# Input and output products of a state-space scan on narrow strips of TensorE: issued together, and copied out of PSUM, inside a one-core encoder block

## The chip, the cores and the metric

The kernel runs on one core of one Trainium2 chip. The metric is the device time in microseconds (us) of one execution. The kernel before was run three times; the median of these runs stands for it. One further execution was taken with the hardware profiler, and all rows below are from that one.

## The reference, cut to what matters

One layer of an encoder with 256 tokens and a width of 2048: a combined input projection feeds three mixers (chunked attention, a diagonal complex state-space scan called S5, and an mLSTM), whose gated results go through an output projection; then come cross-attention to a memory and a SwiGLU block. Everything is float32. The change touches the S5 branch:

```python
u = h[...].reshape(l, 48, 16)                  # 48 groups of 16 channels
bu_r = einsum('lgn,gpn->lgp', u, bbr)          # input products: 16 channels -> 64 states
bu_i = einsum('lgn,gpn->lgp', u, bbi)
x[t] = a * x[t-1] + bu[t]                      # complex, diagonal, over the 256 tokens
y = einsum('lgp,gnp->lgn', xr, c_re) - einsum('lgp,gnp->lgn', xi, c_im)   # output products
y = gelu(y + d_skip * u); y = y * sigmoid(y @ w_glu + b_glu)
```

## The kernel before

The large products (`gemm_i`, `gemm_ii`) are float32 emulated with two float32r parts. For each 1 MB piece of weights SyncE (SP) issues a load into one of two buffers (`raw`); ScalarE casts 1024 columns at a time to `whi` (L116), VectorE computes the rest `wlo` (L117), and TensorE multiplies three times per k-tile (L146 to L148, or L169 to L171 for transposed results). `whi` and `wlo` have four buffers each. These steps have the highest priority of the planner (`WPRI`); evacuations of products have the next one (`EPRI`); all else is ordered by its place in the text.

The S5 branch runs beside that, as a generator (`s5_gen`, L400) from which `run(bg_gen, n)` (L755 to L798) takes one step at a time between the products of the first phase. Its steps: 48 groups are 24 pairs; a pair has 128 states, one per partition. Six chunks `c` hold four pairs `j` each. For a pair, VectorE builds the table `E` of rotations (six operations, L372 to L377), TensorE makes two input products from 32 rows (L422, real and imaginary, each on the row strip `q = 32 * j` of the array) into one PSUM tile of the tag `sm`, VectorE rotates them straight from PSUM (L428, L429, into `s2k` scratch), adds and subtracts (L430, L431), scans (L435, twice) and rotates back into the tile `xx` (L440 to L443; four buffers). After four pairs TensorE makes the eight output products of the chunk (L449): 128 rows to 32 columns, real (`i = 0`) and imaginary (`i = 1`), each pair on its own column strip, and all in one PSUM tile `py`; L451 adds the result to `u`. The output products are asked for in the order `i`, then `j = 0, 1, 2, 3`. After the last chunk `s5_glu` (L454) makes the operand `yg` from `u`.

The tag `sm` has four PSUM banks, which all transposes, the mLSTM and the attention share. TensorE's queue is a fixed list that the planner wrote when the kernel was built: between the large products stand those of the three mixers, where the planner expected their inputs. A float32 product (not float32r) shows in the trace as two records: 48 input products are 96 records on L422, 48 output products 96 records on L449.

Of the kernel before, what the change touches and what calls it, by code (L numbers as in the profile page):

```python
# [14 lines left out]
ALU = mybir.AluOpType  # L15
# [23 lines left out]
# columns of the array of per-partition parameters  # L39
# [8 lines left out]
# columns of the array of constants: identity, ones, mask of the mLSTM  # L48
# [4 lines left out]
def tile_block(ctx: ExitStack, tc: tile.TileContext, a: dict, out: bass.AP):  # L53
# [26 lines left out]
    def junk(tag, n=512):  # L80
        """somewhere for an output that only its sum is wanted of"""
        t = scr.tile([P, 512], BF16, tag=tag, name=nm(tag), bufs=1)
        return t[:, :n]
# [22 lines left out]
    def dma_after(dst, src):  # L106
        """a load that comes behind the weights asked for so far"""
        with tc.issue_after(last_w[0]):
            nc.sync.dma_start(dst, src)
# [10 lines left out]
    def gemm_i(xh, xl, nk, src, off, n, evac, first=None):  # L120
        """acc[tok, n] = x @ w; w comes from the flat array src at off, in blocks [P, 4, n]."""
# [35 lines left out]
    def gemm_ii(xh, xl, nk, src, off, evac, raw=None):  # L157
        """acc[n, tok] = (x @ w)^T for 128 columns of w, in one block [P, nk, 128]."""
        po = acc()[:, :T]
        if raw is None:  # L160
            raw = load_w(src[off:off + P * nk * P].rearrange("(p f) -> p f", p=P), nk * P)
        k = 0
        while k < nk:
            kk = min(8, nk - k)
            hi, lo = split_w(raw, k * P, (k + kk) * P)
            for j in range(kk):
                kt = k + j
                h = hi[:, j * P:(j + 1) * P]
                PE.matmul(po, h, xh[:, kt, :], start=(kt == 0), stop=False)  # L169
                PE.matmul(po, h, xl[:, kt, :], start=False, stop=False)  # L170
                PE.matmul(po, lo[:, j * P:(j + 1) * P], xh[:, kt, :], start=False,  # L171
                          stop=(kt == nk - 1))
            k += kk
        evac(po)
        return off + P * nk * P

# [18 lines left out]
    def rstd_of(dst, ss, n, r=None):  # L195
        """dst = (ss / n + eps) ^ -0.5 (* r, one factor per partition)"""
        w = dst.shape[1]
        G.tensor_scalar(dst, ss, 1.0 / n, EPS, ALU.mult, ALU.add)
        G.tensor_tensor(dst, dst, mhalf[:, 0:w], ALU.pow)
        if r is not None:  # L200
            G.tensor_scalar(dst, dst, r, None, ALU.mult)

    def split_act(hi, lo, src, g=None):
        """hi + lo = src * g, exactly up to float32."""
# [7 lines left out]
    def transposes(dst, srcs):  # L212
        """dst [P, len * 128] in PSUM: each src [rows, 128] transposed."""
        for i, s in enumerate(srcs):
            PE.transpose(dst[:, i * P:(i + 1) * P], s, ident)  # L215
# [8 lines left out]
    # the tensor engine's clock rises while it waits for the first loads  # L224
# [12 lines left out]
    def load_x(k, n=0):  # L237
        """what is wanted of x before the weights of k-tiles k .. k+n-1 of the first product"""
# [20 lines left out]
    def vexp(dst, src, n):  # L259
# [12 lines left out]
        # 2^k in two factors  # L272
# [12 lines left out]
    # =====================  S5  =====================  # L285
# [25 lines left out]
    def s5_params():  # L311
# [5 lines left out]
        # reduce the angle to [-pi, pi]  # L317
# [10 lines left out]
        # (a - 1) / lambda  # L328
# [50 lines left out]
    def powers(tb, c1, s1):  # L379
        """tb[:, :, j, t] = (cos, sin) of t * angle, t < 16; returns nothing."""  # L380
# [4 lines left out]
        for n, m in ((2, 1), (3, 2), (5, 4), (9, 7)):  # L385
            # entries n .. n+m-1 are those 1 .. m turned by entry n-1
# [7 lines left out]
    def s5_powers():  # L394
        powers(eb, sp(CS), sp(SNN))
        # angle of 16 steps: step 15 turned by one more
# [3 lines left out]
    def s5_gen():  # L400
        """the scan, pair of groups by pair of groups; yields after each step of work"""
        for c in range(6):
            js = slice(4 * c, 4 * c + 4)
            xs = []
            for j in range(4):
                jj = 4 * c + j
# [10 lines left out]
                q = 32 * j  # L417
                cb = E[:, 0].unsqueeze(1).to_broadcast([P, 2, T])
                sb_ = E[:, 1].unsqueeze(1).to_broadcast([P, 2, T])
                pb = sm()  # L420
                for i in range(2):
                    PE.matmul(pb[:, i * T:(i + 1) * T], bT[q:q + 32, i, c, :], u[q:q + 32, c, :],  # L422
                              start=True, stop=True, tile_position=(q, 0))
# [3 lines left out]
                w, tm = s2k(), s2k()  # L427
                V.tensor_tensor(two(w), two(pb), cb, ALU.mult)  # L428
                V.tensor_tensor(two(tm), two(pb), sb_, ALU.mult)  # L429
# [7 lines left out]
                xx = s5.tile([P, 512], F32, tag="xx", name=nm("xx"), bufs=4)  # L437
                xs.append(xx)
# [7 lines left out]
            for i in range(2):  # L446
                for j in range(4):
                    q = 32 * j
                    PE.matmul(py[q:q + 32, :], cT[:, i, 4 * c + j, :], xs[j][:, i * T:(i + 1) * T],  # L449
                              start=(i == 0), stop=(i == 1), tile_position=(0, q))  # L450
# [20 lines left out]
    # =====================  mLSTM  =====================  # L471
# [23 lines left out]
    def mqk(h):  # L495
        """q^T and k^T of head h, [e, tok]"""
# [26 lines left out]
    def m_gates():  # L523
        """decays of the mLSTM: a (tok-major), -c (rows), exp(-m) (tok-major)"""
# [27 lines left out]
        V.tensor_tensor(rows[:, 0], rows[:, 1], rows[:, 2], ALU.subtract)      # a  # L552
        V.tensor_tensor_scan(rows[:, 3], on, rows[:, 0], NEG, ALU.mult, ALU.max)  # c
        V.tensor_tensor(rows[:, 1], rows[:, 2], rows[:, 3], ALU.add)           # m
# [68 lines left out]
    # =====================  chunked attention  =====================  # L623
# [60 lines left out]
    # =====================  gates and branches  =====================  # L684
# [3 lines left out]
    def gate(b, n, dst):  # L688
        """sigmoid of the gate's pre-activation, branch b, columns of chunk n, into dst(t)"""
# [37 lines left out]
    # us  # L727
# [9 lines left out]
    # xm  # L737
# [10 lines left out]
    # vm, with the input and forget gates beside head 0  # L748
# [7 lines left out]
    # attention and om  # L756
# [18 lines left out]
    # gates and branches m and a  # L775
# [30 lines left out]
    def to_operand(srcs, dh, dl, k0, gname=None):  # L806
        """srcs: two tiles [128 tok, 512]; their transpose goes to k-tiles k0 .. k0+3"""
# [26 lines left out]
    # =====================  output projection, residual  =====================  # L834
# [41 lines left out]
    # =====================  keys and values of the memory  =====================  # L876
# [4 lines left out]
    def norm_head(po, r, n):  # L881
        """RMS-normalised rows of po * r (r a per-row factor), without the gain"""
# [28 lines left out]
    # x1 operand  # L911
# [12 lines left out]
    # =====================  cross attention  =====================  # L924
# [71 lines left out]
    # =====================  SwiGLU  =====================  # L996
# [34 lines left out]
def _rows(w, widths):  # L1031
    """w [K, N] -> flat: for each run of columns, for each 4 k-tiles, a block [128, 4, n]."""
# [13 lines left out]
def _cols(w):  # L1046
    """w [K, N] -> flat: for each 128 columns, a block [128, K / 128, 128]."""
# [4 lines left out]
def _prep(i):  # L1052
# [15 lines left out]
    # per head [128, q|k, 2, 256]  # L1068
# [8 lines left out]
    # relative-position bias, [q, head, (q tile 0: keys 0..127 | q tile 1: keys 0..255)]  # L1077
# [31 lines left out]
    def pairs(v):  # L1109
        """[48, 64, 16] -> block-diagonal over pairs of groups [128, 24, 32]"""  # L1110
# [25 lines left out]
```

## Time and profile before

| | us |
|---|---|
| median of 3 runs | 2051.26 |
| lowest, highest | 2050.34, 2051.73 |
| span of the profiled execution | 2048.7 |
| TensorE busy in it | 2039.7 |
| VectorE busy | 1251.7 |
| ScalarE busy | 966.0 |

The span runs from the first to the last instruction of the profiled execution. The S5 branch issues its first input product at 172.5 us and its last output product at 714.8 us; its operand `yg` is first multiplied at 759 us. A busy TensorE is one that has a matmul in flight; matmuls overlap, so the time that an instruction costs is read from its start to the start of the next one, not from its duration. TensorE's granted clock is 1.00 in all of these stretches, the upper of its two levels.

### The profile page before, as it was taken

What the parts mean: (1) busy time and instruction counts of PE and PEld (TensorE: products, weight loads), DVE (VectorE), ACT (ScalarE), POOL (GpSimd) and SP (SyncE); (2) the same over time, 40 slices, a digit from 0 to 9 for tenths busy, and PEclk for the clock granted to TensorE, in tenths of its full rate; (3) what the DMA queues carried; (4) which work ended last, traced back from release to release, by engine and by line L of the source; (5) the groups of instructions that cost most, each with busy time, mean ns of one, the idle gap of its engine ahead of it and who ended that gap; (6) DMA issues with size and microseconds to landing.
All of it is one profiled execution on the core that took longest, in us unless ns stands there. A gap on an engine that the chain in (4) does not pass through costs nothing.

```text
span 2048.7 us, 25114 instructions
## 1 busy us (share of the span) xinstructions
PE 2039.7 (100%) x9880; PEld 1670.9 (82%) x9880; DVE 1251.7 (61%) x1804; ACT 966.0 (47%) x1308; POOL 73.7 (4%) x142
## 2 busy tenths in 40 slices
PE   9999999999999999999999999999999999999999
PEld 7998888777777788888888888888888888888887
DVE  7967885769887857645544655445444444444443
ACT  8555556544344445554544545444444444433332
POOL 1001202000000000011000100000000000000000
PEclk9999999999999999999999999999999999999999
DMA  8555455445555555765555444555555555555553
GB/s 309 186 174 165 152 179 186 155 172 174 180 183 188 192 171 195 271 218 175 175 185 185 144 145 164 185 185 185 185 185 185 185 185 185 185 185 195 195 197 132
DMA packets 60406, 377.78 MB, mean 184 GB/s; under 512 B 6912, under 2 KB 8064, under 8 KB 18816
## 3 DMA queue, kind: packets, MB, share of 16 engines
q1 hardware_dynamic: 56880, 367.42, 51.4%
q0 software_dynamic: 2112, 6.82, 1.2%
q10 hardware_dynamic: 1296, 1.95, 0.3%
q8 instruction: 77, 1.26, 0.2%
q14 instruction: 41, 0.34, 0.1%
HBM read 374.06 MB, written 2.10 MB: 184 GB/s over the span
## 4 chain that ended last, share of the span: by engine, by line
PE 99%; DVE 0%; DMA 0%; issue 0%; SPq 0%; ACT 0%; DVEq 0%; ACTq 0%
PE acc L146 29%; PE acc L148 29%; PE acc L147 28%; PE acc L169 2%; PE acc L170 2%; PE acc L171 2%; PE sm L422 1%; PE sm L812 1%; PE sm L952 1%; PE sm L978 1%; PE sm L449 1%; PE sm L215 0%; PE sm L896 0%; DMA raw<-in_w_in_dram 0%; DVE xT_l L210 0%
## 5 line engine op out<-in xcount | busy, mean ns | idle before, releaser
L117 DVE TENSOR_TENSOR wlo<-raw,whi 128x1024 fp32r<-128x1024 f32 (+2 forms) x700 | 834.7, 1194 | 697.7 <-ACT whi L116 694.3
L116 ACT CAST whi<-raw 128x1024 fp32r<-128x1024 f32 (+2 forms) x700 | 715.9, 1025 | 941.3 <-PE acc L148 816.9
L146 PE MATMUL acc<-whi,x2T_h 128*128 128x512 f32 x704 | 281.2, 399 | 0.0
L148 PE MATMUL acc<-whi,x2T_l 128*128 128x512 f32 x704 | 277.9, 395 | 0.0
L147 PE MATMUL acc<-wlo,x2T_h 128*128 128x512 f32 x704 | 277.2, 394 | 0.0
L147 PE MATMUL acc<-wlo,xT_h 128*128 128x512 f32 (+2 forms) x704 | 264.6, 377 | 1.8 <-DVE wlo L117 1.6
L148 PE MATMUL acc<-whi,xT_l 128*128 128x512 f32 (+2 forms) x704 | 265.3, 378 | 0.0
L146 PE MATMUL acc<-whi,xT_h 128*128 128x512 f32 (+2 forms) x704 | 262.4, 377 | 0.2
L148 PEld LDWEIGHTS acc<-whi,x2T_l 128*128 128x128 f32 x704 | 132.2, 188 | 33.4
L147 PEld LDWEIGHTS acc<-wlo,x2T_h 128*128 128x128 f32 x704 | 132.2, 188 | 31.4
L146 PEld LDWEIGHTS acc<-whi,x2T_h 128*128 128x128 f32 x704 | 132.2, 188 | 30.1
L147 PEld LDWEIGHTS acc<-wlo,xT_h 128*128 128x128 f32 x704 | 132.0, 188 | 29.8 <-DVE wlo L117 3.3
L146 PEld LDWEIGHTS acc<-whi,xT_h 128*128 128x128 f32 x704 | 131.5, 188 | 29.6 <-issue 3.2
L148 PEld LDWEIGHTS acc<-whi,xT_l 128*128 128x128 f32 x704 | 132.1, 188 | 27.8 <-issue 1.9
L146 PE MATMUL acc<-whi,hT_h 128*128 128x512 f32 x352 | 139.1, 395 | 0.0
L147 PE MATMUL acc<-wlo,hT_h 128*128 128x512 f32 x352 | 139.1, 395 | 0.0
L148 PE MATMUL acc<-whi,hT_l 128*128 128x512 f32 x352 | 139.0, 395 | 0.0
L148 PE MATMUL acc<-whi,eT_l 128*128 128x512 f32 x256 | 101.6, 397 | 0.0
L147 PE MATMUL acc<-wlo,eT_h 128*128 128x512 f32 x256 | 101.4, 396 | 0.0
L146 PE MATMUL acc<-whi,eT_h 128*128 128x512 f32 x256 | 101.2, 395 | 0.0
L169 PE MATMUL acc<-xT_h,whi 128*128 128x256 f32 x352 | 99.9, 284 | 0.0
L170 PE MATMUL acc<-xT_l,whi 128*128 128x256 f32 x352 | 99.5, 283 | 0.0
(375 smaller groups left out, 2837.0 us busy)
## 6 DMA issues: line engine op xcount, KB each, us to landing
raw<-in_w_gu_dram SPq DMA_DIRECT2D x88, 1024.0 KB, 4.8
raw<-in_w_in_dram SPq DMA_DIRECT2D x68, 1024.0 KB, 4.8
raw<-in_w_down_dram SPq DMA_DIRECT2D x44, 1024.0 KB, 4.7
raw<-in_w_xkv_dram SPq DMA_DIRECT2D x32, 1024.0 KB, 4.7
raw<-in_w_ii_dram SPq DMA_DIRECT2D x22, 1024.0 KB, 5.0
raw<-in_w_out_dram SPq DMA_DIRECT2D x16, 1024.0 KB, 5.0
raw<-in_w_xq_dram SPq DMA_DIRECT2D x16, 1024.0 KB, 4.8
raw<-in_w_xo_dram SPq DMA_DIRECT2D x16, 1024.0 KB, 4.8
```

The lines of the kernel that those rows point to most:

```text
L116: S.copy(hi[:, :n], raw[:, c0:c1])
L117: V.tensor_tensor(lo[:, :n], raw[:, c0:c1], hi[:, :n].bitcast(F32), ALU.subtract)
L146: PE.matmul(o, sh, h, start=(kt == 0), stop=False)
L147: PE.matmul(o, sh, lw, start=False, stop=False)
L148: PE.matmul(o, xl[:, kt, t * P:(t + 1) * P], h, start=False, stop=(kt == nk - 1))
L169: PE.matmul(po, h, xh[:, kt, :], start=(kt == 0), stop=False)
L170: PE.matmul(po, h, xl[:, kt, :], start=False, stop=False)
L171: PE.matmul(po, lo[:, j * P:(j + 1) * P], xh[:, kt, :], start=False, stop=(kt == nk - 1))
L422: PE.matmul(pb[:, i * T:(i + 1) * T], bT[q:q + 32, i, c, :], u[q:q + 32, c, :], start=True, stop=True, tile_position=(q, 0))
L449: PE.matmul(py[q:q + 32, :], cT[:, i, 4 * c + j, :], xs[j][:, i * T:(i + 1) * T], start=(i == 0), stop=(i == 1), tile_position=(0, q))
L812: PE.transpose(px[:, j * T + t * P:j * T + (t + 1) * P], srcs[t][:, (kp + j) * P:(kp + j + 1) * P], ident)
L952: PE.matmul(pS[:, t * T:(t + 1) * T], qx[:, qi, d, t * P:(t + 1) * P], kx[:, ki, d], start=(d + i == 0), stop=(d == 3 and i == 2))
```

## The change

For every second pair (`j` = 0 and 2) the input products of this pair and of the next one are now issued together: four products, real ones of both pairs, then imaginary ones of both, on two neighbouring row strips and into two PSUM tiles. ScalarE copies both tiles to SBUF, into two buffers of `xx`, which are now taken here and not after the scan. VectorE then rotates from and into this SBUF tile; the `s2k` scratch tile `w` is gone. The output products get the priority `EPRI`, and the pairs are asked for in the order 3, 2, 1, 0. No load, no wait by hand and no other line is changed (the rest of the diff takes out comments).

```diff
         for c in range(6):
-            js = slice(4 * c, 4 * c + 4)
             xs = []
             for j in range(4):
+                if j % 2 == 0:
+
+                    pb = [sm(), sm()]
+                    for i in range(2):
+                        for e in range(2):
+                            q = 32 * (j + e)
+                            PE.matmul(pb[e][:, i * T:(i + 1) * T], bT[q:q + 32, i, c, :],
+                                      u[q:q + 32, c, :], start=True, stop=True,
+                                      tile_position=(q, 0))
+                    for e in range(2):
+                        xx = s5.tile([P, 512], F32, tag="xx", name=nm("xx"), bufs=4)
+                        S.copy(xx, pb[e])
+                        xs.append(xx)
                 jj = 4 * c + j
...
-                q = 32 * j
                 cb = E[:, 0].unsqueeze(1).to_broadcast([P, 2, T])
                 sb_ = E[:, 1].unsqueeze(1).to_broadcast([P, 2, T])
-                pb = sm()
-                for i in range(2):
-                    PE.matmul(pb[:, i * T:(i + 1) * T], bT[q:q + 32, i, c, :], u[q:q + 32, c, :],
-                              start=True, stop=True, tile_position=(q, 0))
...
-                w, tm = s2k(), s2k()
-                V.tensor_tensor(two(w), two(pb), cb, ALU.mult)
-                V.tensor_tensor(two(tm), two(pb), sb_, ALU.mult)
+                w, tm = xs[j], s2k()
+                V.tensor_tensor(two(tm), two(w), sb_, ALU.mult)
+                V.tensor_tensor(two(w), two(w), cb, ALU.mult)
...
-                xx = s5.tile([P, 512], F32, tag="xx", name=nm("xx"), bufs=4)
-                xs.append(xx)
+                xx = xs[j]
...
             py = sm()[:, :T]
-            for i in range(2):
-                for j in range(4):
-                    q = 32 * j
-                    PE.matmul(py[q:q + 32, :], cT[:, i, 4 * c + j, :], xs[j][:, i * T:(i + 1) * T],
-                              start=(i == 0), stop=(i == 1), tile_position=(0, q))
+            with tc.high_priority(offset=EPRI):
+                for i in range(2):
+                    for j in (3, 2, 1, 0):
+                        q = 32 * j
+                        PE.matmul(py[q:q + 32, :], cT[:, i, 4 * c + j, :],
+                                  xs[j][:, i * T:(i + 1) * T], start=(i == 0), stop=(i == 1),
+                                  tile_position=(0, q))
```

## Rows read from the trace of the kernel before

**Rows 1.** The page: busy time of each engine (share of the span, instructions), and the chain of work that ended last, by engine.

```profile
PE 2039.7 (100%) x9880; PEld 1670.9 (82%) x9880; DVE 1251.7 (61%) x1804; ACT 966.0 (47%) x1308; POOL 73.7 (4%) x142
...
PE 99%; DVE 0%; DMA 0%; issue 0%; SPq 0%; ACT 0%; DVEq 0%; ACTq 0%
```

**Rows 2.** Busy time of each engine by stretch of the first phase (us from:to, length, then PE, PEld, DVE, ACT and POOL busy with instructions, granted clock, DMA share, GB/s); the last is the sum from 160 to 759 us.

```profile
450.00:560.00 110.00, 110.00 (x475) 82.85 (x475) 100.29 (x165) 46.25 (x47) 1.61 (x3) 1.00 0.51 170
560.00:716.00 156.00, 156.00 (x682) 120.46 (x681) 129.77 (x198) 65.04 (x68) 3.75 (x7) 1.00 0.56 187
...
sum 599.00, PE 597.70 PEld 478.40 DVE 464.89 ACT 293.10 POOL 35.82; mean PE 99.62 PEld 79.73 DVE 77.48 ACT 48.85 POOL 5.97
```

**Rows 3.** What TensorE waited for from 160 to 760 us (total us, times, longest).

```profile
PE sm L449 <- issue: 1.3, 1, 1.3
```

**Rows 4.** TensorE in order of time around the input products of one pair (start us, us, engine, line, operation, records).

```profile
652.14 0.40 PE L147 MATMUL acc<-wlo,xT_h 128*128 128x512 f32 x1
652.38 0.39 PE L148 MATMUL acc<-whi,xT_l 128*128 128x512 f32 x1
652.70 1.13 PE L422 MATMUL sm<-u,s5mats 32*128 32x256 f32 x4
653.76 0.50 PE L146 MATMUL acc<-whi,ya 128*128 128x512 f32 x1
654.10 0.40 PE L147 MATMUL acc<-wlo,ya 128*128 128x512 f32 x1
```

**Rows 5.** The same around the input products of two pairs that the planner had put next to each other.

```profile
688.49 0.39 PE L148 MATMUL acc<-whi,xT_l 128*128 128x512 f32 x1
688.81 1.14 PE L422 MATMUL sm<-u,s5mats 32*128 32x256 f32 x8
689.88 0.50 PE L146 MATMUL acc<-whi,xT_h 128*128 128x512 f32 x1
690.22 0.40 PE L147 MATMUL acc<-wlo,xT_h 128*128 128x512 f32 x1
```

**Rows 6.** The same where three pairs stood next to each other.

```profile
448.42 1.15 PE L422 MATMUL sm<-u,s5mats 32*128 32x256 f32 x12
449.50 0.50 PE L148 MATMUL acc<-whi,xT_l 128*128 128x512 f32 x1
```

**Rows 7.** TensorE in order of time around the output products of the fourth chunk, which stand in two runs: the second one, of five products.

```profile
545.34 0.39 PE L147 MATMUL acc<-wlo,ya 128*128 128x512 f32 x1
545.66 1.05 PE L449 MATMUL sm<-xx,s5mats 128*32 128x256 f32 x10
546.64 0.50 PE L148 MATMUL acc<-whi,ya 128*128 128x512 f32 x1
546.98 0.40 PE L146 MATMUL acc<-whi,ya 128*128 128x512 f32 x1
```

**Rows 8.** The chain from 172 to 716 us: its shares by line, and pieces of it (start us, us, what). L422 has 23 pieces on it: 16 like that at 652.77, three like that at 194.91, two like that at 196.01 (the three of 172.58, 196.01 and 215.88 border on L571, a row-strip product of the mLSTM), one of twelve records and one of eight. L449 has 15: six of ten records (that of the fourth chunk is in rows 7), five of four or six records, like that at 543.10, which is the first run of the same chunk, and four like that at 452.55.

```profile
by line: PE acc L146 26.9%; PE acc L148 26.7%; PE acc L147 26.5%; PE sm L422 4.1%; PE acc L169 2.9%; PE acc L171 2.8%; PE acc L170 2.8%; PE sm L449 2.0%; PE sm L215 1.0%; PE sm L664 0.6%; PE sm L680 0.6%; PE sm L579 0.5%; PE sm L590 0.5%; P
...
194.91 0.62 PE sm L422 x2
...
196.01 0.41 PE sm L422
...
452.55 0.55 PE sm L449 x2
...
543.10 0.56 PE sm L449 x6
...
652.77 1.05 PE sm L422 x4
```

**Rows 9.** Groups of instructions by line (line, engine, operation, out<-in, count, busy us, mean ns, idle us before and what ended it): VectorE's rotations from PSUM (L428) and from SBUF (L440), the cast and the rest of the weights from 172 to 716 us, and ScalarE's copies of a whole PSUM tile to SBUF in the mLSTM (L511, from 100 us on).

```profile
L117 DVE TENSOR_TENSOR wlo<-raw,whi 128x1024 fp32r<-128x1024 f32 x172 | 210.0, 1221 | 92.4 <-ACT whi L116 92.0
L116 ACT CAST whi<-raw 128x1024 fp32r<-128x1024 f32 x172 | 180.6, 1050 | 240.9 <-PE acc L148 203.1 <-PE acc L170 15.2 <-DMA raw<-in_w_in_dram 8.1
L440 DVE TENSOR_TENSOR xx<-s2k,E 128x512 f32<-128x512 f32 x24 | 16.5, 688 | 0.3
L428 DVE TENSOR_TENSOR s2k<-sm,E 128x512 f32<-128x512 f32 x24 | 16.5, 686 | 4.6 <-PE sm L422 4.6
...
L511 ACT COPY mw<-sm 128x512 f32<-128x512 f32 x6 | 3.5, 580 | 1.0 <-PE sm L510 1.0
```

**Rows 10.** What ScalarE waited for, from 450 to 560 us and from 560 to 716 us (total us, times, longest).

```profile
ACT whi L116 <- DMA raw<-in_w_br_m_dram: 2.9, 1, 2.9
...
ACT whi L116 <- PE acc L148: 87.9, 47, 3.7
```

**Rows 11.** The end of the branch: the last operation that makes `yg` on VectorE, and TensorE's first products with it (durations in ns, first and last start in us).

```profile
718.81 0.69 DVE L207 TENSOR_TENSOR yg<-u,yg 128x512 fp32r<-128x512 f32 x1 [1.61 <-ACT yg L206]
...
L169 PE MATMUL acc<-yg,whi x36: 277/280/283, 759.1 to 771.4; 128*128 128x256 f32 x36
```

**Rows 12.** VectorE at the first and the last operation of the last pair, and ScalarE's casts while TensorE has nothing but large products (start us, us).

```profile
695.49 0.42 DVE L372 TENSOR_TENSOR s2k<-ea,eb 128x256 f32<-128x256 f32 x1
...
709.68 0.42 DVE L443 TENSOR_TENSOR xx<-xx,s2k 128x256 f32<-128x256 f32 x1
...
720.12 1.05 ACT L116 CAST whi<-raw 128x1024 fp32r<-128x1024 f32 x1 [0.39 <-PE acc L148]
722.92 1.05 ACT L116 CAST whi<-raw 128x1024 fp32r<-128x1024 f32 x1 [1.75 <-PE acc L148]
```

## The prediction

> **What bounds the kernel now.** I began with the page: TensorE is busy for 2039.7 of 2048.7 us and the chain that ended last is 99% TensorE [rows 1]. A busy TensorE can still be badly fed, so next I read the stretches in which the S5 branch lives: from 160 to 759 us TensorE is busy for 597.7 of 599 us, at a granted clock of 1.00 (the upper of its two levels, 2.4 GHz), beside 464.9 us of VectorE and 293.1 us of ScalarE [rows 2], and its waits there come to one of 1.3 us, ahead of an output product [rows 3]. ScalarE, which feeds it, waits for TensorE to free `whi` (203 of its 241 us of idle time ahead of the casts) [rows 9]. So every microsecond that goes out of TensorE's queue between 172 and 716 us should leave the total, as long as the feed can go faster by as much. That is why the third view is TensorE in order of time: what does an S5 product cost the queue?
>
> **Reading one run.** Large products start 0.233 us apart. Around a lone pair, the L148 at 652.38 is followed only after 0.32 us, the four L422 records take 1.06 us, and the L146 at 653.76 holds the next one back for 0.34 us [rows 4]. From 652.38 to 654.10 is 1.72 us; two large products would have taken 0.47, so the pair costs 1.25 us: 1.06 inside and 0.20 for entering and leaving the strips. Two pairs next to each other cost 690.22 - 688.49 - 0.47 = 1.26 us [rows 5], and three 1.08 us inside [rows 6]. So products on different row strips do run beside each other, and a second pair is nearly free.
>
> **What it removes: input products.** On the chain L422 has 23 pieces: 16 x 1.056 + 3 x 0.62 + 2 x 0.41 + 1.08 + 1.07 = 21.7 us [rows 8] (by its share, 4.1% of 544, 22.3). About 20 of them stand between full-array products and pay 0.20 for the switch; three border on other row-strip products [rows 8]. 21.7 + 4.0 = 25.7 us. After: 12 groups of two pairs x 1.26 = 15.1 us. Gain 10.6 us.
>
> **Output products.** L449 has 15 pieces: 6 x 0.98, five of about 0.57 and four x 0.55, together 10.9 us [rows 8], and 15 x 0.20 for the switches makes 13.9 us. They are scattered since the three products `i = 0, j = 0..2` go early and the other five once pair 3 is done; the imaginary products of pairs 0 to 2 go no earlier, although their inputs are ready, so the order of the text inside `py` is kept [rows 7, 8]. Asked for as 3, 2, 1, 0, the first one waits for the last pair and all eight stand in one run. What does a run of eight cost? The run of five has four records on strip 3 (both products of pair 3) and two on each other strip, and takes 0.98 us inside, 546.98 - 545.34 - 0.47 = 1.17 us in all [rows 7]. A run of eight has four records on each strip. If strips run beside each other, 0.98 again; if they didn't at all, the run of three, 0.56 us [rows 8], comes on top. I take 0.98, because the row with four strips active is the nearest: 6 x 1.18 = 7.1 us. Gain 6.8 us (6 x 0.56 = 3.4 less at the far end).
>
> **What it adds.** 24 copies on ScalarE, 512 columns from PSUM: L511 is this operation, 0.58 us [rows 9], so 13.9 us beside an engine that is busy for half of these stretches and idles because TensorE is not done [rows 2, 9, 10]; cost nothing on the path. If that cover were gone, 13.9 us. VectorE rotates from SBUF rather than PSUM: 686 against 688 ns [rows 9], no difference in either direction; the operations are as many as before. Nothing is issued on SP's or POOL's queues that was not before, and no load moves past another.
>
> **The waits that it adds.** VectorE's first rotation now waits for a copy on top of the product: some 0.6 us later per group, while it has the six operations for `E` and the `wlo` to do. In TensorE's queue the output run waits for pair 3, and behind it stand the large products; the trace has one such wait in 15, 1.3 us [rows 3]. It may vanish or come again elsewhere: I take 0, bounds -1.3 and +2.6. On ScalarE the copies of a chunk's first two pairs wait until the previous chunk's output run has freed `xx`; the casts stand behind them, and TensorE waits for those. I take 0 for it, since casts run ahead: it is the slower rival. PSUM: a group needs two of the four `sm` banks at once. If only one is free, the group falls apart. Before, some pairs were cut up within themselves [rows 8]; I allow for one group in twelve, 1.2 us. The branch as a whole may end later: `yg` is done at 719.5 and wanted at 759.1 [rows 11], 40 us of slack, 17 of which the faster TensorE takes.
>
> **A rule that speaks against it.** The row above has ScalarE idle ahead of the casts for 241 us [rows 9], so 13.9 us of copies fit. The Trainium skill, TensorEngine Tiling (Array Packing), section PSUM Bottleneck, says that packing makes TensorE faster but not the emptying of PSUM, which can then become the limit. By the row the copies cost 0, by the rule up to 13.9 us, which would eat nearly all of the gain; it is the third rival below.
>
> **The sum.** -10.6 - 6.8 + 1.2 = -16.2 us. The profiled execution spans 2048.7 us, 2.6 under the median of 2051.3; all of the change lies inside the span, so I take the 2.6 us as they are: 2048.7 - 16.2 + 2.6 = **2035.1 us**, 0.8% less. At best (no group cut, the old wait gone, a few groups merging into longer runs as in [rows 6]) 2031; with the output run at its far end and two more waits 2041.
>
> **The rivals.**
> - *Groups fall apart.* Two banks of `sm` are seldom free together, so half of the groups go as two lone pairs: 6 x 1.26 + 12 x 1.25 = 22.6 us, a gain of 3.1 + 6.8 = 9.9 us: 2041.4. All of them: 24 x 1.25 = 30.0 us, 4.3 worse than before, net -2.5: 2048.8. This is also the case in which the change does not do what it says. For it: attention and mLSTM want the same banks. Against: a copy empties a bank in 0.58 us, where before VectorE came to it when it could, and half of the chunks run after the attention is over.
> - *The feed takes the place of TensorE.* VectorE is busy for 100.3 of 110 us at 450 and 129.8 of 156 at 560 [rows 2], and ScalarE already waits for a load for 2.9 us there [rows 10]; if the copies come on top of that, up to 13.9 us come back: 2049.0. Against: no large product waits for `whi` or `wlo` in the whole stretch [rows 3], and VectorE at 230 us of 256 (266 less some 10) would be at 90%.
> - *Slower: copies that block ScalarE's queue.* If the planner puts a chunk's first copies a whole pair too early, ScalarE stands for a pair's time on VectorE, 695.5 to 710.1 = 14.6 us [rows 12]. TensorE has three buffers of weights in hand, 2.80 us each, less a cast of 1.05 and a rest of 1.23 [rows 9, 12]: 6.1 us. It would wait for 8.5 us at each of five chunk boundaries, 42.5 us: 2077.6. The gain is gone from a block of 6.1 + 16.2 / 5 = 9.3 us on. For it: the queues are fixed lists written from estimates. Against: the same estimates put output products into TensorE's queue right after the same VectorE work, and of 15 runs one was too early, by 1.3 us [rows 3].
>
> **How the numbers follow.** Likeliest case, 2035.1: 0.73. Groups fall apart by half, 2041.4: 0.12; wholly, 2048.8: 0.04. Feed, 2049.0: 0.05. Blocked queue, 2077.6: 0.06. The range takes in the likeliest case with its bounds and the half-cut groups: 2031 to 2043, leaving out 0.15. A measurement of this kernel tells about 0.2%, 4.1 us, from no change: faster 0.85 (the first two), same 0.09, slower 0.06.
>
> **What would show it.** Right: L422 in about 12 runs of eight records, 1.07 us inside; L449 in six runs of 16 records of about 1 us; TensorE without new waits between 172 and 716 us; the large products after the branch earlier by some 16 us, and nothing else moved. Wrong: runs of four records (banks), output runs of 1.5 us (strips that don't overlap), waits of L146 or L147 for `whi` or `wlo` (feed), or ScalarE's copies with long waits for L449 ahead of a wait of TensorE (blocked queue).

## The result, and the profile after

The changed kernel takes **2039.70 us** (median of 4 runs, 2038.49 to 2040.35), the kernel before 2051.49 us beside it (median of 4, 2050.34 to 2052.85). The ratio is 0.9943, 95% interval 0.9929 to 0.9957: faster by 11.8 us. Forecast were 2035.1 us and a gain of 16.2 us, so about three quarters of the gain came. The profiled execution spans 2036.7 us, 12.0 less than that of before, and it is the shortest of the four runs.

First the page of the changed kernel: busy time of each engine, and the chain that ended last by engine (before: [rows 1]).

```profile
PE 2025.7 (99%) x9880; PEld 1666.2 (82%) x9880; DVE 1251.8 (61%) x1804; ACT 975.1 (48%) x1332; POOL 78.6 (4%) x142
...
PE 96%; DVE 1%; POOL 1%; DMA 1%; ACT 1%; issue 0%; SPq 0%; DVEq 0%; POOLq 0%; ACTq 0%
```

TensorE has 14.0 us less work with the same 9880 instructions, which is what the overlap of strips should look like; ScalarE has 24 instructions more, the copies. But TensorE's share of the chain fell from 99 to 96%: somewhere it now waits for others (back from such a wait the chain goes over the engine that was late, though TensorE was mostly busy beside it), and the span shrank by 2.0 us less than its work did.

Next, TensorE in order of time around a group of two pairs (start us, us, engine, line, operation, records; L411 are the input products).

```profile
501.53 0.40 PE L147 MATMUL acc<-wlo,xT_h 128*128 128x512 f32 x1
501.76 0.40 PE L148 MATMUL acc<-whi,xT_l 128*128 128x512 f32 x1
502.09 1.13 PE L411 MATMUL sm<-u,s5mats 32*128 32x256 f32 x8
503.15 0.50 PE L146 MATMUL acc<-whi,ym 128*128 128x512 f32 x1
503.49 0.40 PE L147 MATMUL acc<-wlo,ym 128*128 128x512 f32 x1
```

From 501.76 to 503.49 are 1.73 us for eight records, less 0.47 for two large products: 1.26 us, as in [rows 5], where a lone pair took 1.25 [rows 4]. And the same view around an output run (L456).

```profile
540.36 0.39 PE L146 MATMUL acc<-whi,ya 128*128 128x512 f32 x1
540.68 1.07 PE L456 MATMUL sm<-xx,s5mats 128*32 128x256 f32 x16
541.68 0.50 PE L147 MATMUL acc<-wlo,ya 128*128 128x512 f32 x1
542.02 0.40 PE L148 MATMUL acc<-whi,ya 128*128 128x512 f32 x1
```

All eight output products take 1.00 us inside (540.68 to 541.68), where five took 0.98 [rows 7]. The chain from 172 to 716 us (start us, us, what; before: [rows 8]) has six such output runs, eleven input runs of eight records, and one group that fell apart into two runs of four:

```profile
371.00 1.00 PE sm L456 x16
...
372.49 1.05 PE sm L411 x4
...
374.91 1.05 PE sm L411 x4
...
454.08 1.06 PE sm L411 x8
...
483.57 1.00 PE sm L456 x16
484.57 1.06 PE sm L411 x8
```

So the input products have 11 x 1.06 + 2 x 1.05 = 13.8 us instead of 21.2, and the output products 6.0 instead of 10.9. At 483.57 the input run follows the output run at once, so that this place is entered and left only once; this occurs again at 246.22.

What TensorE waited for from 130 to 760 us (total us, times, longest; before: [rows 3]) shows where the rest went.

```profile
PE acc L169 <- DVE ev L625: 2.1, 1, 2.1
PE sm L613 <- ACT t2k L609: 1.0, 3, 0.4
PE sm L554 <- DVE g_az L551: 0.2, 1, 0.2
```

The old wait ahead of an output product is gone. The new long one is TensorE standing ahead of a large product until VectorE's `om_evac` operation (L625) has emptied an accumulator. Around it, TensorE in order of time, with what the second product waited for in brackets:

```profile
238.52 0.28 PE L171 MATMUL acc<-xT_h,wlo 128*128 128x256 f32 x1
240.87 0.38 PE L169 MATMUL acc<-xT_h,whi 128*128 128x256 f32 x1 [2.07 <-DVE ev L625]
```

VectorE in that stretch: L625 stands behind a `wlo`, which itself waited 1.65 us for its cast, and four operations of the scan.

```profile
237.38 1.23 DVE L117 TENSOR_TENSOR wlo<-raw,whi 128x1024 fp32r<-128x1024 f32 x1 [1.65 <-ACT whi L116]
238.52 0.68 DVE L446 TENSOR_TENSOR xx<-s2k,E 128x512 f32<-128x512 f32 x1
239.13 0.69 DVE L447 TENSOR_TENSOR s2k<-s2k,E 128x512 f32<-128x512 f32 x1
239.73 0.42 DVE L372 TENSOR_TENSOR s2k<-ea,eb 128x256 f32<-128x256 f32 x1
240.06 0.42 DVE L373 TENSOR_TENSOR s2k<-ea,eb 128x256 f32<-128x256 f32 x1
240.40 0.42 DVE L625 TENSOR_TENSOR ev<-acc,rb 128x256 f32<-128x256 f32 x1
```

And ScalarE just before: the cast (L116) stands behind a row scaling of the mLSTM (L609) that waited 1.14 us for GpSimd.

```profile
235.94 0.47 ACT L609 ACTIVATE t2k<-sm,mq 128x256 f32<-128x256 f32 x1 [1.14 <-POOL mq L201]
236.31 1.04 ACT L116 CAST whi<-raw 128x1024 fp32r<-128x1024 f32 x1
```

Last, the copies and the first rotation by line from 172 to 716 us (count, busy us, mean ns, idle us before and what ended it; before: [rows 9]).

```profile
L435 DVE TENSOR_TENSOR s2k<-xx,E 128x512 f32<-128x512 f32 x24 | 16.5, 688 | 2.6 <-ACT xx L416 2.2
L416 ACT COPY xx<-sm 128x512 f32<-128x512 f32 x24 | 13.0, 586 | 6.2 <-PE sm L411 6.2
```

Copies of 586 ns and rotations of 688 ns, as forecast, and VectorE waits 2.2 us in all for the copies.

To compare kernels I divided TensorE's time from the start of its last q/k product of the mLSTM to the start of its first product with `yg`. A record's time is the distance to the next start, and what a large product takes over its usual distance next to small products is counted as the switch. The large products are as many in every kernel and are counted at their usual distances, 551.5 us in each. In us:

| kernel | length | input runs | output runs | their switches | other small products, with switches | waits | large, over 551.5 |
|---|---|---|---|---|---|---|---|
| before | 625.1 | 21.2 | 10.9 | 5.6 | 34.0 | 1.3 | 0.7 |
| after | 613.2 | 13.8 | 6.0 | 2.7 | 35.0 | 3.3 | 1.0 |
| after less before | -11.9 | -7.4 | -4.9 | -2.9 | +1.0 | +2.0 | +0.3 |

### The profile page after: what moved, and what is told of

The parts are those of the page before. It is cut to its first block, busy times and chain, and to the rows that moved or that the text cites. A ratio compares the mean times of both kernels' runs of the same rounds, so it can differ in the third digit from the quotient of the medians.

```text
span 2036.7 us, 25145 instructions
## 1 busy us (share of the span) xinstructions
PE 2025.7 (99%) x9880; PEld 1666.2 (82%) x9880; DVE 1251.8 (61%) x1804; ACT 975.1 (48%) x1332; POOL 78.6 (4%) x142
## 3 DMA queue, kind: packets, MB, share of 16 engines
q8 instruction: 77, 1.26, 0.3%
## 4 chain that ended last, share of the span: by engine, by line
PE 96%; DVE 1%; POOL 1%; DMA 1%; ACT 1%; issue 0%; SPq 0%; DVEq 0%; POOLq 0%; ACTq 0%
PE acc L146 28%; PE acc L148 28%; PE acc L147 28%; PE acc L170 2%; PE acc L169 2%; PE acc L171 2%; PE sm L820 1%; PE sm L411 1%; DMA raw<-in_w_in_dram 1%; PE sm L960 1%; PE sm L986 1%; DVE wlo L117 1%; PE sm L904 0%; PE sm L215 0%; PE sm L456 0%
## 5 line engine op out<-in xcount | busy, mean ns | idle before, releaser
L117 DVE TENSOR_TENSOR wlo<-raw,whi 128x1024 fp32r<-128x1024 f32 (+2 forms) x700 | 834.6, 1194 | 685.7 <-ACT whi L116 683.0
L116 ACT CAST whi<-raw 128x1024 fp32r<-128x1024 f32 (+2 forms) x700 | 715.1, 1025 | 911.6 <-PE acc L148 742.2
```

The source lines that it names most:

```text
L116: S.copy(hi[:, :n], raw[:, c0:c1])
L117: V.tensor_tensor(lo[:, :n], raw[:, c0:c1], hi[:, :n].bitcast(F32), ALU.subtract)
```

## Experiments

The theory was that the gain is the overlap of strips and the fewer runs, and that what is missing against the forecast was lost to waits in TensorE's queue. The rivals: the copies cost or bring something of their own; the priority, not the order, makes the output runs; the two parts bring the same thing twice. Each kernel's median is compared with runs of the kernel before on the same chip.

**The new input side alone** (groups and copies; the output products in their old order without priority).

```
-            with tc.high_priority(offset=EPRI):
-                for i in range(2):
-                    for j in (3, 2, 1, 0):
...
+            for i in range(2):
+                for j in range(4):
```

> The new input side (products of two pairs together, copies by ScalarE, rotation from SBUF), with the output products asked for as before (i, then j = 0 to 3, no priority). By the sum: the input side is worth 7.4 us inside its runs and about 1.3 us of switches, the output side 4.9 and 1.6. Theory (TensorE's queue time adds up, and the new waits of about 3 us before 240 us come with the copies): 2051.5 - 8.7 + 3 = 2045.8, and the profile shows waits of TensorE between 150 and 250 us like those of the changed kernel. Rival (the new waits come with the output run): 2042.8 and no such waits.

Measured: 2045.84 against 2050.87 us, ratio 0.9975 (0.9966 to 0.9985), a gain of 5.0 us. In TensorE's queue the input runs fell to 15.5 us (nine groups whole, two in halves and one cut six and two), the output runs stayed near the old 10.9 at 10.4, and the waits rose to 2.1.

**The new output side alone** (in the kernel before).

```
-            for i in range(2):
-                for j in range(4):
...
+            with tc.high_priority(offset=EPRI):
+                for i in range(2):
+                    for j in (3, 2, 1, 0):
```

> The kernel before with the output products asked for as 3, 2, 1, 0 at the higher priority; input products and rotations as before. Theory: 2051.5 - 6.5 = 2045, L449 in six runs of 16 records of 1.00 us, and hardly a wait of TensorE in the first phase. Rival (the output run brings the waits): 2048 with waits of about 3 us between 150 and 250 us.

Measured: 2041.73 us against the same 2050.87, ratio 0.9958 (0.9945 to 0.9970), a gain of 9.1 us, more than its own 4.9 us of output runs: the input runs fell too, from 21.2 to 19.1, and all switches from 5.6 to 3.4, because lone pairs came to stand next to each other or right behind an output run. It has no copy, and yet it has a wait at the same operation (TensorE's waits, 130 to 760 us; L619 here is `om_evac`'s):

```profile
PE acc L169 <- DVE ev L619: 1.6, 1, 1.6
```

The two gains sum to 14.2, the whole change brings 11.8: they overlap, and their waits don't cancel. Set against the output side alone, the whole change is 0.9943 beside 0.9958, some 3 us, and the two intervals overlap. So in the time, what the input side adds on top of the output side is not clear of the noise; that it is there is read from the trace, 13.8 us of input runs against 19.1.

**Each pair alone, with its copy** (output side as changed).

```
-                if j % 2 == 0:
-                    pb = [sm(), sm()]
...
+                q = 32 * j
+                pb = sm()
...
+                S.copy(xx, pb)
```

> The changed kernel with each pair's input products issued for itself again, then copied by ScalarE; output run as changed. Theory: the input products cost 25 us of TensorE's queue again where they stand alone, so 2039.7 + 8.7 = 2048; where the planner happens to put two pairs side by side, that pair's 1.25 us is not lost. Rival (the gain came from the copies emptying PSUM, not from the strips): 2040.

Measured: 2042.78 us, ratio 0.9959 (0.9946 to 0.9973), input runs 18.8 us. The 2048 of its theory did not come: as in the run before it, three runs of two pairs and one of three stand side by side without having been asked for. Against the output side alone (0.9958, 19.1 us) it differs in the text by the copies and the rotations out of SBUF that go with them: these cost nothing and bring nothing by themselves that could be measured.

**Groups without copies** (VectorE rotates out of PSUM; `xx` allocated afterwards).

```
-                    for e in range(2):
-                        xx = s5.tile([P, 512], F32, tag="xx", name=nm("xx"), bufs=4)
-                        S.copy(xx, pb[e])
...
+                V.tensor_tensor(two(w), two(pb[j % 2]), cb, ALU.mult)
+                V.tensor_tensor(two(tm), two(pb[j % 2]), sb_, ALU.mult)
```

> Both parts of the change, but without the 24 copies: VectorE rotates straight from the two PSUM tiles of a group into scratch, as before. Theory (the copies on ScalarE, or the rotation from SBUF beside GpSimd's small operations, bring the new waits): 2037, no wait of TensorE over 0.5 us between 160 and 250 us, and GpSimd's operations of the mLSTM as short as in the kernel before. Rival (the waits come from where the planner puts the steps, whatever they are): 2039 to 2043, with waits elsewhere. A second rival, that two banks held until VectorE comes starve the others: groups fall apart, 2043 or more.

Measured: 2043.04 us, ratio 0.9959 (0.9947 to 0.9972). That is in the rival's range, with waits elsewhere, but the interval overlaps that of the whole change, so this settles nothing on the time. In its trace nine groups stay whole instead of eleven (input runs 15.5 us), one output run is cut in two, and TensorE has other waits, none of them at `om_evac`:

```profile
PE sm L610 <- ACT t2k L606: 2.7, 2, 1.4
```

Its profiled execution also lost time to the clock, which fell to the lower of its two levels while the second of these waits lasted; four of its five runs show a mean clock of 0.998 or 0.999. The same kind of window as further down (us from:to, length, busy time of PE, PEld, DVE, ACT and POOL, granted clock, DMA share, GB/s):

```profile
241.00:245.00 4.00, 4.00 (x27) 2.82 (x20) 4.00 (x11) 0.85 (x3) 0.00 (x0) 0.50 0.67 210
```

**Each copy twice** (a second one to a scratch tile).

```
                         S.copy(xx, pb[e])
+                        S.copy(junk("jke"), pb[e])
```

> The changed kernel with every copy of ScalarE made twice, the second time into a scratch tile that nobody reads: 24 more operations of some 0.6 us. Theory (ScalarE waits for TensorE anyway, so the copies are covered): 2039.7, within 2 us. Rival (copies come back in the time, as the rule on emptying PSUM has it): half or more of 14 us, 2047 to 2054.

Measured: 2038.17 against 2051.16 us, ratio 0.9936 (0.9923 to 0.9950). Another 14.4 us on ScalarE, as its lines from 172 to 716 us show, cost nothing:

```profile
L417 ACT CAST jke<-sm 128x512 bf16<-128x512 f32 x24 | 14.4, 598 | 0.0
L416 ACT COPY xx<-sm 128x512 f32<-128x512 f32 x24 | 14.2, 590 | 7.3 <-PE sm L411 7.3
```

**Both pairs of a group on one strip** (same products in number and size, no overlap between the two).

```
-                            q = 32 * (j + e)
+                            q = 32 * j
```

> The changed kernel with both pairs of a group on the row strip of the first one (the second pair gets the first pair's input channels, so this leaves out half of the input products' real work while every instruction stays). Theory (different row strips run beside each other): the eleven runs of eight records go from 1.06 to about 8 x 0.216 + 0.1 = 1.83 us, 8.4 us more: 2048. Rival (what counts is only that the products stand next to each other, with fewer switches): runs of 1.06 us, 2040.

Measured: 2048.76 (11 runs) against 2051.16 us, ratio 0.9989 (0.9980 to 0.9998). TensorE in order of time:

```profile
507.31 0.40 PE L148 MATMUL acc<-whi,xT_l 128*128 128x512 f32 x1
507.64 1.99 PE L411 MATMUL sm<-u,s5mats 32*128 32x256 f32 x8
509.56 0.50 PE L146 MATMUL acc<-whi,ym 128*128 128x512 f32 x1
```

Eight records on one strip take 1.92 us (507.64 to 509.56), on two strips 1.06. Its input runs take 23.2 us in all, 9.4 more than after, which is what eleven such runs bring. The overlap of the strips is the gain of the input side; standing next to each other is not enough.

**The old order with the priority.**

```
-                    for j in (3, 2, 1, 0):
+                    for j in range(4):
```

> The changed kernel with the output products asked for in the old order 0, 1, 2, 3, but at the new priority. Theory (it is the order that makes one run of eight, since the first product in line has to wait for the last pair): output runs scattered as in the kernel before, 10 us and more inside and 2 of switches, where the changed kernel has 6.0 and 0.8: 2045. Rival (the priority makes the run): 2039.7 with runs of 16 records.

Measured: 2048.38 (11 runs) against 2050.78 us, ratio 0.9989 (0.9980 to 0.9998). The output products stand in 16 runs, of 2, 4, 6, 10 and only once 16 records, 11.4 us in all. Pieces of its chain:

```profile
591.86 0.56 PE sm L456 x4
...
607.93 0.55 PE sm L456 x2
...
622.68 0.98 PE sm L456 x10
```

The priority alone does not make one run: the order, with the last pair first, is needed. The new order without the priority was not run, so that the order would be enough by itself is not shown. The scattered output products also pull input groups apart (17.1 us).

**No steps of the scan in the mLSTM stage** (the whole branch later; the second rival's question, how much slack VectorE has).

```
         m_core(h)
-        run(bg_gen, 1)
```

> The changed kernel with the scan's four steps taken out of the mLSTM stage (they follow in the later steps). Theory (the 3.3 us of waits come from scan steps put into the crowded mLSTM stage, where ScalarE, VectorE and GpSimd stand in a chain): waits of TensorE from 150 to 250 us under 0.7 us, 2037. Rival (the mLSTM's own chain makes them, wherever the scan stands): 2039.7 with waits of 2 to 3 us. Second rival: the branch uses up its slack of 37 us and the products with yg wait for it: 2042 or more.

Measured: 2044.79 against 2051.16 us, ratio 0.9970 (0.9959 to 0.9982). The waits between 130 and 250 us are gone, and another stands at the end of the branch, where the large products are used up and the last output run waits for the last pair on VectorE (L448 is that pair's last operation but one):

```profile
746.63 1.93 PE L456 MATMUL sm<-xx,s5mats 128*32 128x256 f32 x16 [3.93 <-DVE xx L448]
```

So slack is what covers VectorE in the changed kernel, where `yg` is done long before its use (the tile's instructions: line, count, durations in ns, first and last start in us):

```profile
L169 PE MATMUL acc<-yg,whi x36: 277/279/283, 747.1 to 759.3; 128*128 128x256 f32 x36
...
L207 DVE TENSOR_TENSOR yg<-u,yg x3: 686/686/693, 708.0 to 709.9; 128x512 fp32r<-128x512 f32 x3
```

From 709.9 to 747.1 are 37 us; the kernel before had 40 [rows 11]. The run of 16 above takes 1.93 us instead of 1.00; the stretch by window (us from:to, length, then PE, PEld, DVE, ACT and POOL busy with instructions, granted clock, DMA share, GB/s) says why:

```profile
746.00:753.00 7.00, 5.64 (x36) 4.38 (x37) 4.16 (x8) 4.25 (x7) 0.00 (x0) 0.56 0.19 61
```

The clock is near its lower level after the wait, and TensorE's work goes at about half the speed there.

**The same with groups of four pairs.**

```
-                if j % 2 == 0:
-                    pb = [sm(), sm()]
+                if j == 0:
+                    pb = [sm() for _ in range(4)]
...
-                        for e in range(2):
-                            q = 32 * (j + e)
+                        for e in range(4):
+                            q = 32 * e
...
-        run(bg_gen, 1)
```

> As the late start, with the input products of all four pairs of a chunk issued together on four row strips and four PSUM tiles. Theory (a further strip costs 0.01 us): at most six input runs of 16 records and 1.09 us, so 13.8 + 1.9 becomes 7.7 us, and less waiting: 2030 to 2033. Rival (four banks are seldom free at once, the groups fall apart where attention and mLSTM want them): 2037 to 2041.

Measured: 2044.27 us, ratio 0.9965 (0.9952 to 0.9977), slower than either forecast. The input runs take 11.3 us instead of 14.4, and the wait at the end of the branch grows to 5.7 us: what TensorE saves it waits for, once VectorE's last pair is what ends last.

**The row factors of the mLSTM without GpSimd** (three small operations on VectorE in their place).

```
-            rstd_of(q[:, 3:4], q[:, 2:3], MD, q[:, 1:2])
+            V.tensor_scalar(q[:, 3:4], q[:, 2:3], 1.0 / MD, EPS, ALU.mult, ALU.add)
+            V.reciprocal(q[:, 3:4], q[:, 3:4])
+            V.tensor_scalar(q[:, 3:4], q[:, 3:4], q[:, 1:2], None, ALU.mult)
```

> The changed kernel with the mLSTM's row factors made on VectorE instead of GpSimd, with a reciprocal in place of the power -0.5 (this leaves out the square root, so the mLSTM's output is scaled otherwise). Theory (the waits before 240 us come from the mLSTM's chain over GpSimd, whose small operations stretch beside VectorE's operations on two SBUF tiles, and from what stands behind it on ScalarE): waits of TensorE from the mLSTM stage to the first product with yg fall from 3.3 to under 1.2 us, 2037. Rival (the planner's places make them, whatever engine the chain runs on): 2 to 4 us of waits, 2039.

Measured: 2037.77 against 2050.78 us, ratio 0.9937 (0.9923 to 0.9951). The wait at `om_evac` is gone; 1.4 us for L609's operation and 0.8 ahead of an output run are there instead.

**Groups of two in the first three chunks, of four in the last three.**

```
+                m = 2 if c < 3 else 4
+                if j % m == 0:
+                    pb = [sm() for _ in range(m)]
...
+                        for e in range(m):
```

> The changed kernel with groups of two pairs in the first three chunks and of four pairs in the last three, which run after the attention is done with its PSUM banks. Theory (a further strip costs 0.01 us, and banks are free then): three input runs fewer, 3 x 1.26 = 3.8 us: 2036. Rival (a chunk's four copies wait together for the output run, VectorE gets the scan's input later and TensorE waits for the branch): 2040 or more, with waits ahead of L456 or of the products with yg.

Measured: 2039.43 us, ratio 0.9942 (0.9929 to 0.9954). Input runs 11.7 us, a group of four costs 1.08 us inside, hardly more than one of two. But waits rise to 4.6 us and the large products by 2.1 against after: at 240.56 the wait at `om_evac` is there again, and behind it the lower clock. Windows of this kernel, and TensorE in order of time:

```profile
238.00:241.00 3.00, 0.91 (x7) 0.70 (x7) 3.00 (x8) 2.58 (x3) 0.00 (x0) 1.00 0.30 113
241.00:245.00 4.00, 4.00 (x23) 4.00 (x22) 4.00 (x10) 0.58 (x2) 0.00 (x0) 0.57 0.00 0
245.00:249.00 4.00, 4.00 (x43) 3.23 (x43) 4.00 (x11) 1.66 (x3) 0.00 (x0) 1.00 0.70 233
```

```profile
240.56 0.39 PE L169 MATMUL acc<-xT_h,whi 128*128 128x256 f32 x1 [2.09 <-DVE ev L625]
```

4.0 x (1 - 0.57) = 1.7 us go to the clock.

**The same with a shorter GpSimd chain** (of its three operations only the power stays there).

```
-            rstd_of(q[:, 3:4], q[:, 2:3], MD, q[:, 1:2])
+            V.tensor_scalar(q[:, 3:4], q[:, 2:3], 1.0 / MD, EPS, ALU.mult, ALU.add)
+            G.tensor_tensor(q[:, 3:4], q[:, 3:4], mhalf[:, 0:1], ALU.pow)
+            V.tensor_scalar(q[:, 3:4], q[:, 3:4], q[:, 1:2], None, ALU.mult)
```

> The kernel with groups of four pairs in the last three chunks, with the mLSTM's row factors shortened on GpSimd: of its three small operations only the power stays there, the other two go to VectorE (the same result). Theory (the wait of 2.1 us ahead of a large product near 240 us comes from that chain, and TensorE's clock falls after it in part of the executions): no wait over 1.5 us there, clock 1.00 in all executions, 2039.4 - 2 - 1 = 2036.5. Rival (the waits only move): 2 us or more of waits elsewhere in the mLSTM stage, 2038 to 2040, with the clock at 1.00 only if none of them is as long as 2 us.

Measured: 2037.74 against 2050.86 us, ratio 0.9934 (0.9920 to 0.9947), the lowest median of all the versions, though its interval overlaps that of the change. The input runs take 11.3 us, 2.5 less than after, and that is where its gain stands; its waits sum to 5.3 us, 2.0 more than after. Its wait at `om_evac` is as long as ever. In this kernel the `wlo` ahead of it does not wait for a cast, and VectorE works from 236 to 241 us without a pause, so the wait does not need GpSimd's chain in front of it (though the power is still made there):

```profile
PE acc L169 <- DVE ev L627: 2.4, 1, 2.4
```

## Why the prediction was right, and what it missed

The sign, the mechanism and the range held; the gain was 4.4 us too large. Its terms against the table above (the forecast's cut group, 1.2 us, counted as 1.06 inside and 0.14 of switch):

| term | forecast | measured |
|---|---|---|
| inside the input runs | 21.7 to 13.8: -7.9 | 21.2 to 13.8: -7.4 |
| inside the output runs | 10.9 to 5.9: -5.0 | 10.9 to 6.0: -4.9 |
| switches of both | 7.0 to 3.7: -3.3 | 5.6 to 2.7: -2.9 |
| waits | 0 | +2.0 |
| other small products and their switches | 0 | +1.0 |
| large products | 0 | +0.3 |
| sum | -16.2 | -11.9 |

- **What bounds the kernel** held: 14.0 us less of TensorE's busy time left the span but for the waits.
- **Input products**: 11 whole groups of 12, one apart, exactly as allowed, each at the price of [rows 5]. That the strips overlap is shown by the runs on one strip, 1.92 against 1.06 us.
- **Output products**: six runs of eight at 1.00 us, the end of the bound that the prediction took. That the priority alone does not make them is shown by the old order with the priority; order and priority together make them in the kernel before as well (the output side alone). The order alone was not run.
- **Switches**: 0.20 each, read off an isolated pair, was too much for the mean. The 38 runs of before paid 5.6 us, 0.15 each. The isolated runs above still pay 0.20; those that stand next to another small product can't pay all of it. This over-counted the gain by 0.4 us; with 0.5 on the input runs and 0.1 on the output runs it makes 1.0 of the 4.4 us. Waits make 2.0, other small products 1.0 and large ones 0.3.
- **The term that missed most is "I take 0" for the new waits**, with bounds of -1.3 and +2.6 that were meant for the output run. The old wait did vanish, but 3.3 us came elsewhere: at a large product of the mLSTM stage behind `om_evac`, and at that stage's own transposes. I had looked for new waits at the products that were moved and at the weights, not at others that share VectorE's and ScalarE's fixed order with the branch. +2.0 lies within the bounds, which is luck in part, since they were drawn for another place; with all of the branch's work re-ordered 0 was the wrong value to take.
- **Copies cost 0** held: twice as many cost nothing, and lone pairs with a copy take what lone pairs without one take. The rule of the Trainium skill, TensorEngine Tiling (Array Packing), section PSUM Bottleneck, that emptying PSUM can become the limit, is not borne out here: 28.6 us of emptying (14.4 + 14.2) fit beside TensorE. The prediction hands this rule to its third rival, but the 13.9 us that it gives for it stand in the second one, the feed.
- **The blocked queue** and **the feed** did not come: no large product waits for `whi` or `wlo` in the list of waits above. The slack at the end of the branch was mis-sized: of 40 us the prediction let the faster TensorE take 17, but 37 are left, since `yg` is made earlier too (its last operation starts at 709.9 against 718.81 us [rows 11]). Moved later, the branch ends 3.9 us too late for TensorE.
- **Outside the sum**, the clock. Two of the four runs show a mean granted clock of 0.999 and took 2040.1 and 2040.4 us, the other two 1.000 and 2038.5 and 2039.3. The runs of the kernel with each copy twice all show 1.000. In the version with groups of two and four the trace shows 1.7 us lost after a wait of 2.1, and in that with both pairs on one strip the clock is 0.57 from 242 to 246 us, behind the same wait of 2.1. That the same stretch cost the runs of the changed kernel their 1 to 2 us is argued from this, since its profiled execution was one at 1.000.

**What stays open** is why the wait comes. It stands in versions with copies and without (the output side alone), with groups and without, and with a short GpSimd chain; it is gone where the scan's early steps are gone, where the copies are doubled or left out, and where GpSimd has no part. Each of these also changes the fixed order of VectorE's and ScalarE's queues, and no run changed the order alone. The rows show where the time goes in the changed kernel: ahead of `om_evac` stand four operations of the scan, 1.88 us (238.52 to 240.40), nearly the whole wait. But with the output side alone one operation of the scan stands there, and the wait is 1.6 us. So I read it as a matter of that order, which any edit to the branch draws anew: over the versions in which the branch does not end too late, all of TensorE's waits sum to between 1.6 and 5.3 us, against 1.3 in the kernel before. This is argued, not shown.

## What to carry to other kernels

Where TensorE is the bound and small products use a quarter of its rows or columns, look in the trace for two of them that already stand side by side on different strips: their price is that of the change, and here it held to 0.01 us (1.26 forecast and found). A run held together here when the operand that comes last was asked for first, at a raised priority; the priority alone left it scattered. Count what the edit does to every queue that it re-orders, not only to the instructions that it moves: a wait of 2 us at an unrelated product, and in some executions, as argued above, the clock after it, took 2 to 4 us of the 15 that the branch itself gained.

## What the runs showed of the hardware that I had not expected

Around waits of a few us TensorE's granted clock was at its lower level, 1.2 GHz, for most of the next few us in some executions: 0.57 over 4 us behind a wait of 2.1, 0.56 over 7 us at the end of one of 3.9, and 0.50 over 4 us behind two of 1.4 and 1.3 (rows above). In the changed kernel's profiled execution the same wait of 2.07 us was followed by the full clock:

```profile
241.00:245.00 4.00, 4.00 (x35) 4.00 (x35) 4.00 (x11) 1.96 (x4) 0.00 (x0) 1.00 0.00 0
```

So it was after 2.4 us in the version with the shorter GpSimd chain. A short wait can thus cost nearly its own length again; what decides it no run here shows.

Small GpSimd operations stretch beside VectorE. GpSimd while VectorE stands idle, and beside a VectorE operation, in the changed kernel:

```profile
170.28 0.19 POOL L198 TENSOR_SCALAR mq<-mq 128x1 f32<-128x1 f32 x1
...
1123.16 0.86 POOL L198 TENSOR_SCALAR nh<-nh 128x1 f32<-128x1 f32 x1 [1.11 <-ACT jke L894]
1124.10 0.57 POOL L199 TENSOR_TENSOR nh<-nh,mhalf 128x1 f32<-128x1 f32 x1
```

```profile
1122.76 1.21 DVE L117 TENSOR_TENSOR wlo<-raw,whi 128x1024 fp32r<-128x1024 f32 x1
1123.89 0.68 DVE L207 TENSOR_TENSOR t2k<-sm,t2k 128x512 fp32r<-128x512 f32 x1
```

The same operation takes 0.19 us alone and 0.86 when it begins inside `wlo`'s L117, and it ends 0.05 us after it (1124.02 against 1123.97). Beside L207, one of whose inputs lies in PSUM, L199 takes its usual 0.57. The Trainium skill, SBUF — State Buffer, section Who interferes with whom, says that a VectorE operation with two SBUF inputs contends with a GpSimd operation that reads SBUF, and that the ports they share are held by an exclusive lock; these rows agree. The change gives the first rotations two SBUF inputs in place of one in PSUM, and GpSimd's busy time rose from 73.7 to 78.6 us. That this had a share in the time is not shown: without GpSimd in that chain the ratio was 0.9937, inside the interval of the change.
